# One decoder layer on eight cores: a build-time list scheduler, one matmul less per attention tile, and no activation-table switches

## The chip, the cores and the metric

The kernel runs on all eight cores of one Trainium2 chip, two dies of four cores. Each core does two of the sixteen sequences, with its own copy of the weights and no exchange. The time of one execution is that of its slowest core, in device microseconds (us).

Executions come in two states. In the fast one all cores have the same granted TensorE clock. In the slow one the cores of one die, sometimes of both, show a lower clock and run some per cent longer. Kernels are compared here by their fast executions. Where a kernel had none, I take the die that stayed at its normal clock in a slow execution ("undisturbed die"): for kernels that have both, the two agree to within 0.2%.

PE is TensorE, PEld its weight load, DVE VectorE, ACT ScalarE, POOL GpSimd, SP SyncE. "Clock" is the mean granted TensorE clock, 1.00 being full speed. In a row of groups or of the timeline, L492 is line 492 of that kernel's file, and "out<-in" are the program's names.

## The reference, cut to what matters

```python
xn = rms_norm(h, mix_norm)                       # h: (16, 4096, 1024) float32
z  = xn @ w_in                                   # b, c, u (512 each), q, k, v (512 each), f (8)
y_conv = gate_b * causal_depthwise_conv(gate_c * u, conv_w)       # width 3
log_f  = log_sigmoid(z_f + b_f)
c      = cumsum(log_f)                           # per head, along the sequence
s      = q.k / 8 + c[t] - c[s]                   # causal
y_attn = softmax(s) @ v                          # 8 heads x 64
y  = group_rms_norm(concat(y_conv, y_attn))      # over groups of 64 channels
h  = h + y @ w_o
h  = h + (silu(g) * up) @ w_down                 # g, up = rms_norm(h) @ w_gate_up, 2816 wide
h  = h + sigmoid(rms_norm(h) @ w_ple_gate + b) * (p @ w_ple_proj)
return rms_norm(h)
```

The softmax's denominator is never needed: the group norm that follows takes any factor of a row out again. What matters for time is the term c[t] - c[s]. Its part in s (the key) is one number per partition when a score tile has keys on partitions and queries along the row, so it can be the bias of the exponential. Its part in t (the query) varies along the row. That is the "decay row".

## The kernel before: the parts that matter here

A core works through sixteen blocks of 512 tokens, eight per sequence. The Python loop emits a block's operations in the order of the formula, and each engine executes them in that order: norm, q, k, v, convolution with its group norm, attention, output projection, norm, FFN, norm, embedding gate, final norm.

```python
class Prog:
    def op(self, eng, fn, reads=(), writes=()):       # appended to the engine's queue at once
        deps = self._deps(reads, writes)
        self.cnt[eng] += 1
        tok = (eng, self.cnt[eng])
        self.q[eng].append((fn, deps, None))
        self._update(tok, reads, writes)
        return tok
# ... (cut: DMA, emission with semaphores, constants, buffers)
            # attention: one unit is a head x a tile of 128 keys x 512 queries
            for i in range(len(units) + LOOK):                     # LOOK = 3
                if i < len(units):
                    h, kt, c0, dg, first, last = units[i]          # dg: tile on the diagonal
                    def fqk(e, ...):
                        e.matmul(PS[sbk][:, c0:T], lhsT=KT[:, hp, kt * 128:(kt + 1) * 128],
                                 rhs=QT[:, h, c0:T], start=True, stop=False)
                        ins = e.matmul(PS[sbk][:, c0:T], lhsT=sel[:, h * 128:(h + 1) * 128],   # decay row
                                       rhs=crow[:, c0:T], start=False, stop=(not dg))
                        if dg:
                            ins = e.matmul(PS[sbk][:, c0:c0 + 128], lhsT=identb[:], rhs=maskb[:],
                                           start=False, stop=True)
                        return ins
                    P.op("pe", fqk, ...)
                    P.op("act", lambda e, ...: e.activation(out=Pb[pi][:, c0:T], in_=PS[sbk][:, c0:T],
                         func=AF.Exp, bias=cK[:, kt, h:h + 1], scale=1.0), ...)
                j = i - LOOK
                if j >= 0:
                    P.op("pe", lambda e, ...: e.matmul(PS[ob][0:65, c0:T], lhsT=VA[:, kt, h, :],
                         rhs=Pb[pi][:, c0:T], start=first, stop=last), ...)
# ... (cut: group norm of a head: Square, matmul, Ln, Exp(-0.5 x), multiply; odd heads are moved
#      to partitions 64 to 127 by one more matmul with a shift matrix)
            norm_to_xnT(hb, 8)                                     # root by Ln, then Exp, on ACT
            for (f_lo, f_n, gu, dn) in pl["ffn"]:
                for j in range(f_n):
                    mm_fm(bg, gv, BG, (j % 2) * 128)
                    mm_fm(bu, gv, BG, 256 + (j % 2) * 128)
                    P.op("act", lambda e, ...: e.activation(out=sg[si][:], in_=PS[bg][:], func=AF.Silu), ...)
                    P.op("dve", lambda e, ...: e.tensor_tensor(out=actT[:, j, :], in0=sg[si][:],
                         in1=PS[bu][:], op=ALU.mult), ...)
```

## Time and profile before

| | before |
|---|---|
| median of the first 4 executions | 6063 us (5842 to 6454) |
| fast execution, slowest core | 5842 us |
| profiled core: TensorE busy, idle | 5043 us, 798 us |
| mean clock, fast execution | 0.924 |
| activation-table loads | 65 of 1283 ns |
| share of the weights' DMA queue | 45% of 16 engines |

The prediction below shows the page's head and three stretches of one block. Four more rows of the page's costliest groups (busy us and mean ns of one, then the idle time of that engine just before them and what ended it) carry an argument that it missed:

```profile
L722 ACT ACTIVATE P<-ps,cK 128x512 bf16<-128x512 f32 (+3 forms) x2304 | 1341.5, 650 | 92.6 <-PE ps L715 69.3
...
L713 PE MATMUL ps<-QT,KT 128*128 128x512 bf16 (+3 forms) x2304 | 846.9, 368 | 101.9 <-DVE acc L637 101.9
L732 PE MATMUL ps<-P,VA 128*65 128x512 bf16 (+3 forms) x2304 | 841.0, 365 | 43.6 <-ACT P L722 15.9
L715 PE MATMUL ps<-crow,sel_s 128*128 128x512 bf16 (+3 forms) x2304 | 845.7, 367 | 0.0
```

L713, L715 and L732 are the three matmuls of an attention unit (scores, decay row, values), L722 its exponential. Matmuls overlap in the record, so the mean of 367 ns is not their spacing: that is 0.217 us when dense, 0.65 us for the three of a full tile.

The slices of DVE and ACT (each digit the busy tenths of 1/40 of the span), which show the engines taking turns:

```profile
DVE  3242423222230240331242323241312402313113
ACT  3142342625428148258242524336262382572662
```

### The profile page before, as it was taken

Reading aid. Unit: us, or ns where it says so; the run is one execution under the profiler, and the core shown is the slowest. Engines: PE = TensorE matmul, PEld = TensorE weight load, DVE = VectorE, ACT = ScalarE, POOL = GpSimd, SP = SyncE. Lnnn points to the kernel's source line nnn. Section 1 sums busy time; section 2 is a strip of 40 time slices with the busy share of each in tenths; the row PEclk is TensorE's granted clock in tenths of the full one; section 3 lists DMA queues with packets and bytes.
Section 4 is the critical chain, followed back from the end, with each engine's and each line's share of the span. In section 5 each row is a group of like instructions: output and inputs, shape, how many; then the busy total and the mean of one; then the engine's idle time right before and its main releaser. Section 6 shows DMA issues by size and latency. Waiting matters only on the chain.

```text
span 5840.9 us, 76877 instructions; the slowest of 8 cores (5820.6 to 5840.9 us)
## 1 busy us (share of the span) xinstructions
PE 5043.0 (86%) x24128; PEld 2316.7 (40%) x24128; DVE 1629.1 (28%) x2492; ACT 2552.1 (44%) x4663; POOL 270.7 (5%) x509
## 2 busy tenths in 40 slices
PE   5978788898889989889979798888889899898898
PEld 2433334343444334434434343334444344344443
DVE  3242423222230240331242323241312402313113
ACT  3142342625428148258242524336262382572662
POOL 0000000000000000000000000000000000000000
PEclk9989899998999989999989898989999899899999
DMA  5756638174370650740747474562725607417225
GB/s 106 118 109 105 123 60 153 26 131 86 69 144 15 114 114 3 137 89 6 134 95 133 91 126 100 92 135 43 133 53 102 126 3 137 89 31 127 56 36 111
DMA packets 101977, 534.92 MB, mean 92 GB/s; under 512 B 12768, under 2 KB 21344, under 8 KB 60640
## 3 DMA queue, kind: packets, MB, share of 16 engines
q0 software_dynamic: 72720, 453.75, 45.2%
q1 hardware_dynamic: 28880, 76.26, 3.9%
q8 instruction: 222, 3.64, 0.3%
q14 instruction: 155, 1.27, 0.1%
HBM read 950.13 MB, written 33.55 MB: 168 GB/s over the span
## 4 chain that ended last, share of the span: by engine, by line
PE 69%; DVE 13%; ACT 8%; issue 6%; DMA 4%; DVEq 0%; ACTq 0%; POOL 0%; POOLq 0%
PE ps L492 29%; PE ps L732 8%; PE ps L713 7%; PE ps L715 7%; PE ps L817 7%; DMA wslot<-wpack 4%; DVE xnT L484 4%; PE ps L767 2%; PE ps L771 2%; DVE acc L869 1%; PE ps L543 1%; DVE h L873 1%; ACT acc L867 1%; PE ps L857 1%; ACT sqb L736 1%
## 5 line engine op out<-in xcount | busy, mean ns | idle before, releaser
L492 PE MATMUL ps<-xnT,wslot 128*128 128x512 bf16 x8192 | 1909.5, 397 | 73.8 <-DVE xnT L484 54.3
L722 ACT ACTIVATE P<-ps,cK 128x512 bf16<-128x512 f32 (+3 forms) x2304 | 1341.5, 650 | 92.6 <-PE ps L715 69.3
L492 PEld LDWEIGHTS ps<-xnT,wslot 128*128 128x128 bf16 x8192 | 827.8, 102 | 1136.5 <-issue 259.4
L713 PE MATMUL ps<-QT,KT 128*128 128x512 bf16 (+3 forms) x2304 | 846.9, 368 | 101.9 <-DVE acc L637 101.9
L732 PE MATMUL ps<-P,VA 128*65 128x512 bf16 (+3 forms) x2304 | 841.0, 365 | 43.6 <-ACT P L722 15.9
L715 PE MATMUL ps<-crow,sel_s 128*128 128x512 bf16 (+3 forms) x2304 | 845.7, 367 | 0.0
L817 PE MATMUL ps<-wslot,actT 128*128 128x512 bf16 x2816 | 612.9, 379 | 46.6 <-DVE actT L799 46.6
L382 POOL DMA_DIRECT2D wslot<-wpack x496 | 265.6, 538 | 5522.6 <-PE ps L492 2159.9
L797 ACT ACTIVATE sqb<-ps 128x512 bf16<-128x512 f32 x176 | 105.2, 598 | 834.5 <-PE ps L492 834.4
L817 PEld LDWEIGHTS ps<-wslot,actT 128*128 128x128 bf16 x2816 | 273.2, 98 | 386.3 <-issue 61.5
L732 PEld LDWEIGHTS ps<-P,VA 128*65 128x65 bf16 x2304 | 252.4, 110 | 429.8 <-issue 360.2
L477 PE MATMUL ps<-identb,xnbf 128*128 128x128 bf16 x1536 | 152.5, 262 | 233.7 <-DVE xnT L484 146.9
L444 ACT ACTIVATE junk<-h 128x1024 bf16<-128x1024 f32 x132 | 139.1, 1054 | 448.2 <-DVE h L822 232.9
L715 PEld LDWEIGHTS ps<-crow,sel_s 128*128 128x128 bf16 x2304 | 227.5, 99 | 246.0 <-issue 14.2
L797 ACT ACTIVATE sg<-ps 128x512 bf16<-128x512 f32 x176 | 105.2, 598 | 489.1 <-PE ps L492 489.1
L822 DVE TENSOR_TENSOR h<-h,ps 128x512 f32<-128x512 f32 x256 | 175.9, 687 | 482.9 <-PE ps L817 482.9
L713 PEld LDWEIGHTS ps<-QT,KT 128*128 128x128 bf16 x2304 | 227.2, 99 | 207.9 <-issue 122.0
L857 PE MATMUL ps<-wslot,xnT 128*128 128x512 bf16 x1024 | 269.3, 411 | 22.7 <-DVE pT L840 15.6
L799 DVE TENSOR_TENSOR actT<-sqb,ps 128x512 bf16<-128x512 bf16 x176 | 121.1, 688 | 557.0 <-PE ps L492 540.2
L685 DVE SCALAR_TENSOR_TENSOR yTa<-ps,gattn_s,rs 64x512 bf16<-64x512 f32 x64 | 47.5, 743 | 773.5 <-ACT rs L682 773.5
L799 DVE TENSOR_TENSOR actT<-sg,ps 128x512 bf16<-128x512 bf16 x176 | 121.1, 688 | 488.6 <-PE ps L492 488.6
L689 DVE SCALAR_TENSOR_TENSOR ytmp<-ps,gattn_s,rs 64x512 bf16<-64x512 f32 x64 | 47.5, 742 | 715.8 <-ACT rs L682 380.4
(102 smaller groups left out, 3579.4 us busy)
## 6 DMA issues: line engine op xcount, KB each, us to landing
wslot<-wpack POOLq DMA_DIRECT2D x320, 1024.0 KB, 12.9
wslot<-wpack POOLq DMA_DIRECT2D x64, 768.0 KB, 7.2
wslot<-wpack POOLq DMA_DIRECT2D x64, 640.0 KB, 8.5
h<-x SPq DMA_DIRECT2D x64, 512.0 KB, 19.8
y<-h SPq DMA_DIRECT2D x64, 512.0 KB, 9.0
wslot<-wpack POOLq DMA_DIRECT2D x48, 512.0 KB, 7.1
pin<-p SPq DMA_DIRECT2D x64, 128.0 KB, 4.9
gfin_s<-gfin SPq DMA_DIRECT2D x1, 512.0 KB, 10.1
```

The costliest lines, as they stand in the source:

```text
L382: P.dma("pool", lambda e, o=o, i_=i_: e.dma_start(out=o, in_=i_), f"w{s_}", writes=wr)
L484: P.op("dve", lambda e, pbv=pbv, gb=gb, tt=tt: e.tensor_tensor(out=xnT[:, :, tt * 128:(tt + 1) * 128], in0=pbv.rearrange("p (k t) -> p k t ...
L492: ins = e.matmul(PS[b][:], lhsT=wv[:, kc, c0:c0 + 128], rhs=xnT[:, kc, :], start=(kc == 0), stop=(kc == 7))
L713: e.matmul(PS[sbk][:, c0:T], lhsT=KT[:, hp, kt * 128:(kt + 1) * 128], rhs=QT[:, h, c0:T], start=True, stop=False)
L715: ins = e.matmul(PS[sbk][:, c0:T], lhsT=sel[:, h * 128:(h + 1) * 128], rhs=crow[:, c0:T], start=False, stop=(not dg))
L722: P.op("act", lambda e, sbk=sbk, pi=pi, c0=c0, kt=kt, h=h: e.activation(out=Pb[pi][:, c0:T], in_=PS[sbk][:, c0:T], func=AF.Exp, bias=cK[:, ...
L732: P.op("pe", lambda e, ob=ob, kt=kt, h=h, pi=pi, c0=c0, first=first, last=last: e.matmul(PS[ob][0:65, c0:T], lhsT=VA[:, kt, h, :], rhs=Pb[ ...
L797: P.op("act", lambda e, bg=bg, si=si: e.activation(out=sg[si][:], in_=PS[bg][:], func=AF.Silu), reads=[Bps[bg]], writes=[Bsg[si]])
L799: P.op("dve", lambda e, bu=bu, si=si, j=j: e.tensor_tensor(out=actT[:, j, :], in0=sg[si][:], in1=PS[bu][:], op=ALU.mult), reads=[Bsg[si], ...
L817: ins = e.matmul(PS[b][:], lhsT=actT[:, j, tt * 128:(tt + 1) * 128], rhs=rhs, start=(j == 0), stop=(j == na + nb - 1))
L822: P.op("dve", lambda e, b=b, hh=hh, dh=dh: e.tensor_tensor(out=hh[:, dh * 512:(dh + 1) * 512], in0=hh[:, dh * 512:(dh + 1) * 512], in1=PS[ ...
L857: e.matmul(PS[bgt][:], lhsT=xnT[:, kc, tt * 128:(tt + 1) * 128], rhs=pgv[:, kc, :], start=(kc == 0), stop=False)
```

## The change

The intent has three parts. First, the order of the instructions no longer follows the program: each operation gets a priority ("key") and an estimated duration, and a list scheduler, run while the kernel is built, lays attention and convolution of block n+1 between FFN, embedding and final norm of block n, and the projections of block n+2 at block n's end. Second, the decay row leaves the full tiles. Third, every function on ACT comes from one table set, so that the mixing costs no table loads. The diff's core, with cuts marked:

```diff
+    def op(self, eng, fn, dur, key, reads=(), writes=(), after=(), sem=None, nbytes=0):
+        ...                                   # records the operation, places nothing
+    def schedule(self):
+        ...                                   # per engine: of the ready operations the lowest key,
+        ...                                   # else the one that is ready first; buffers are
+        ...                                   # allotted here; engines and the DMA are simulated
@@ attention, full tiles
-    e.matmul(PS[sbk][:, c0:T], lhsT=KT[...], rhs=QT[...], start=True, stop=False)
-    ins = e.matmul(PS[sbk][:, c0:T], lhsT=sel[...], rhs=crow[:, c0:T], start=False, stop=(not dg))
+    ins = e.matmul(st.ap()[:, c0:T], lhsT=KT[...], rhs=QT[...], start=True, stop=not dg)
+    if dg:
+        e.matmul(st.ap()[:, c0:T], lhsT=sel[...], rhs=crow[:, c0:T], start=False, stop=False)
@@ attention, once per head: before the diagonal tiles are added, multiply by exp(decay of the query)
+    if ui == blk * 4 and blk:
+        P.op("dve", lambda e, ...: e.tensor_tensor(out=o.ap()[0:65, :], in0=o.ap()[0:65, :],
+                                                   in1=et.ap()[0:65, :], op=ALU.mult), ...)
@@ roots: Exp of the float's bits as a first guess, then a polynomial on DVE, instead of Ln and Exp
-    P.op("act", ... func=AF.Ln, scale=1.0 / D, bias=EPS)
-    P.op("act", ... func=AF.Exp, scale=-0.5)
+    P.op("act", ... in_=m.bitcast(I32), func=AF.Exp, scale=SEED_SCALE, bias=SEED_BIAS)
+    P.op("dve", ...)                          # five tiny operations after it, one before
@@ FFN (sigmoid of the embedding gate likewise)
-    P.op("act", ... func=AF.Silu)
+    P.op("act", ... func=AF.Tanh, scale=0.5)
+    P.op("dve", ... scalar_tensor_tensor(out=tb, in0=th, scalar=1.0, in1=PS g, op0=add, op1=mult))
@@ the shift of odd heads
-    P.op("pe", lambda e, ...: e.matmul(PS[g2][:, :], lhsT=shiftm[:, :], rhs=ytmp[:, :], ...))
+    dst = yTa[64:128, h // 2, :]              # DVE writes the upper half itself
@@ weights: 8 slots of 2048 columns instead of 4 of 4096; PSUM: 3 banks scores, 2 output, 3 all else
@@ the order: low key first
+    for n in range(-2, NB):
+        b = float(n)
+        if n >= 0:
+            load_h(n, b - 0.15)
+            wo(n, b + 0.0, b + 0.06)
+        if 0 <= n + 1 < NB:
+            conv(n + 1, b + 0.15, b + 0.7)
+            attention(n + 1, b + 0.0, b + 0.9)
+        if n >= 0:
+            ...                               # norm tiles, b + 0.06
+            ffn(n, b + 0.07, b + 0.68)
+            ...                               # norm tiles, b + 0.68
+            ple(n, b + 0.70, b + 0.80)
+            finish(n, b + 0.80)
+        if n + 2 < NB:
+            qkv(n + 2, b + 0.78, b + 1.0)
```

## The prediction

> **What bounds the kernel now.** I read the cores first: all eight lie within 0.4% of each other, so one core may stand for the chip, and the profile fell in a fast execution (5842 us; the other three took 5998, 6128 and 6454). Then the busy times and the forty slices.
>
> ```profile
> span 5840.9 us, 76877 instructions; the slowest of 8 cores (5820.6 to 5840.9 us)
> ...
> PE 5043.0 (86%) x24128; PEld 2316.7 (40%) x24128; DVE 1629.1 (28%) x2492; ACT 2552.1 (44%) x4663; POOL 270.7 (5%) x509
> ...
> PE   5978788898889989889979798888889899898898
> ...
> PEclk9989899998999989999989898989999899899999
> DMA  5756638174370650740747474562725607417225
> ```
>
> TensorE is the only engine near full. But no slice stays full: it dips, the clock dips with it, and ACT, DVE and DMA take turns. Three stretches of one block, read in the windows view, say why (columns: busy us and count of PE, weight loads, DVE, ACT, POOL, then clock, DMA share, GB/s):
>
> ```profile
> 4860.00:4920.00 60.00, 58.58 (x272) 26.24 (x271) 12.85 (x19) 6.58 (x11) 4.75 (x9) 1.00 0.84 144
> 4980.00:5040.00 60.00, 48.94 (x242) 23.62 (x243) 25.74 (x46) 16.46 (x34) 1.58 (x3) 0.85 0.70 162
> 5100.00:5160.00 60.00, 58.08 (x286) 27.20 (x285) 2.23 (x3) 58.43 (x101) 0.00 (x0) 1.00 0.00 1
> ```
>
> The first is FFN: PE dense at clock 1.00, ACT nearly idle, DMA at 84%. The third is attention: PE dense at 1.00, ACT just as full with exponentials, DMA idle. The middle one is norm, projection and convolution: PE idles a fifth of the time and the clock falls to 0.85. So the limit is PE, plus small serial chains at stage borders that leave it idle and then slow. The waits of PE, longest first, show the chains:
>
> ```profile
> PE ps L477 <- DVE xnT L484: 146.9, 96, 4.2
> PE ps L713 <- DVE acc L637: 101.9, 16, 6.8
> PE ps L477 <- DVE xnbf L460: 85.4, 33, 30.3
> PE ps L696 <- DVE ytmp L689: 81.2, 58, 2.8
> PE ps L644 <- ACT sqb L611: 65.8, 32, 3.1
> ```
>
> Norm transposes, the convolution's last multiply, the shift of odd heads, the group norm: each is PE waiting for a vector or scalar chain with no other PE work queued. The chain of waits agrees: PE is 69% of it, DVE 13%, ACT 8%, DMA only 4%.
>
> To split the span I need PE's work at full clock. In a dense FFN stretch 160 matmuls of 512 columns take 34.7 us: 0.217 us each. Work in units of such a matmul, from the code: per 512-token block 96 for q, k, v, 96 for the convolution's projections, 64 output projection, 528 FFN, 88 embedding gate, 16 for means and shifts, so 888, times 16 blocks 14,208; attention's 1792 full tiles take 3 each (scores, decay row, values), 5376; 512 diagonal tiles of mean width 320 take 3 x 0.625, 960, and masks 128; 1664 transposes a quarter each, 416. Sum 21,088 x 0.217 = 4575 us, and about 50 for small fp32 and 8-column matmuls: 4625. The span is thus 4625 of work, 5841 - 5043 = 798 of idle, and the rest, about 418, of matmuls stretched by the lower clock.
>
> **What the Trainium skill says.** "TensorE: Matmul & The Clock Gate", Part 1: the array runs at half clock until it has been busy for a window of about 3.4 us, and falls back after idling. The trace agrees: the first matmuls after the start follow each other at 0.43 us, dense ones at 0.217. The same page, "Seeing it yourself": a current limit takes a die to 13/16 of the clock when three or more of its cores run dense matmuls. This profile doesn't show it: dense stretches on eight cores have 1.00. The slower executions may be it; I can't tell from a fast profile. "ScalarE: Activation LUTs", Table sets: exp and tanh share a set, ln and exp another, and a switch needs a load. The trace has 65 loads of 1283 ns, 83 us in all. "SBUF — State Buffer", Who interferes with whom: VectorE in its two-port modes locks GpSimd out, and with it the descriptors of GpSimd's DMAs. No row here shows such a stall.
>
> **The change part by part.** It turns the kernel's order over to a list scheduler that runs when the kernel is built. Operations carry a priority and an estimated duration; each engine's static order comes from that simulation. Attention of block n+1 and its convolution are laid beside FFN, embedding and final norm of block n.
>
> 1. Decay row. For full tiles the second matmul (decay of the query) goes; exp of it multiplies the accumulated output once per head before the diagonal tiles. Gone: 1792 x 0.217 = 389 us of PE, all on the path, since attention is PE-dense. Added: 8 matmuls, 8 ACT exponentials (0.59 each) and 8 DVE multiplies (0.69) in 14 blocks: 24 us of PE.
>
> 2. Odd-head shift: 64 matmuls gone, 14 us; its 81 us of waits go too. The convolution's epsilon row adds 64 back. V and the embedding gate run as 256-column halves: same columns, 3072 instructions; as 128-column transposes run at 66 ns in the trace when warm, I add 30 us for small-matmul loss.
> PE work after: 14,208 + 112 + 3584 + 960 + 128 + 416 = 19,408 x 0.217 = 4211, plus 50 and 30: 4290 us. That is 335 less than before.
>
> 3. Tables. Silu and sigmoid become tanh; ln/exp roots become an exponential of the float's bits plus two polynomial corrections on DVE. All but one or two of the 65 table loads go (83 us of ACT), which is what makes interleaving exp and FFN possible.
>
> 4. DVE pays. Per block, with rows' durations: norms 12 x (0.75 + 1.22 + about 0.85 for six tiny operations), 34; 12 group roots at 4 x 0.72 + 0.75 final, 44; convolution's products 4 x 3.4, 13; FFN 22 x 1.4, 31, and down-projection sums 16 x 0.72, 12; embedding 8 x 1.44, 12; output sums 5.5; gate logarithm by polynomial, 26 x 0.26, 7; casts of q, k, v 8; decay multiply 5.5; final norm 4 x 2.1, 8; chaining gaps of 0.1 us, 10. About 190 us, or 3040 in all against 1629.
>
> 5. ACT: 83 us fixed per block and 22 x blk for exponentials, so 2560, unchanged (loads and Ln out, tanh equal to silu, new exponentials in).
>
> 6. DMA: the same weights in half-size pieces, double the slots, all issues including x and y on GpSimd's queue, x read twice. Busy share before is 49% of 5841, 2870 us; 34 MB more at the 76 MB per 228 us of the old queue add 100: 2970.
>
> 7. Idle. Of 798 idle plus 418 clock loss, most sits at borders that now have the other block's matmuls to fill them. What cannot be filled: start (38 us until the first projection, as before), the first block's projection, convolution and attention with no FFN beside them (about 40), the last block's norms and output (about 25). I call it 100. Within the middle I allow 5 to 6% of 4290, 240 us, for in-order queues meeting durations the scheduler did not foresee.
>
> Sum in a fast execution: 4290 + 100 + 240 = 4630, that is 0.79 of 5842.
>
> **The rivals.**
> DVE becomes the bound in light blocks. With blk = 0 PE has about 888 + 75 + 8 units, 210 us; DVE 190, 90% of it, in order, on three PSUM banks shared by FFN, convolution and norms. For: FFN's gate now needs ACT, then DVE, then DVE before its banks are free. Against: at blk = 7 PE has 310 us. If every light block (four of sixteen) went to 240 us and the next four lost 15, I would see 4630 + 150 = 4780.
> DMA becomes the bound: 2970 us of 4630 is 64%, in light blocks 185 of 210. One GpSimd queue with x, y and weights in order could hold a load behind a store. Against: smaller pieces, and demand spread over the whole block instead of bursts at 84%. It would add to the same light blocks, 4750 to 4850.
> The clock: if eight denser cores trip the limit of 13/16, 4290 / 0.8125 = 5280, and the time is 5300 to 5400, still under before's fast time. Against: 1.00 in all dense stretches of this profile.
> The optimistic one: the scheduler fills almost all, 3% loss: 4290 + 100 + 130 = 4520.
>
> **Range and chances.** Fast 4630. The median of before's executions is 1.04 of its fast one; a kernel with a larger share of dense matmuls will suffer a slow die at least as much, so its median may be 1.04 to 1.06, 4815 to 4910. I predict 4740, between the fast time and such a median. The range 4450 to 5150 holds the optimistic and both stall rivals, and a moderately slow state; only the full clock limit falls outside. Even that is faster than before, so faster by over 2%: 0.96; within 2%: 0.02; slower: 0.02, for an order that serializes on a wait I have not seen.
>
> **What would show it.** Right: PE at 94% or more of the span in the middle; clock near 1.00 in a fast execution; slices of ACT and DVE level instead of taking turns; matmuls of the decay row only in diagonal tiles; one or two table loads; DVE near 3000 us, ACT near 2550; the chain of waits over 85% PE. Wrong: PE holes ended by DVE operations of the gate product or root correction in each sequence's first blocks (DVE bound); holes ended by weight transfers (DMA bound); clock at 0.81 on all cores while PE is full (current limit); or PE work well over 4290, which would mean that short matmuls cost more than I took.

## The result, and the profile after

The changed kernel took 5055 us (median of 12 executions, 4833 to 5585), the kernel before 5998 us (median of 17). Its fast executions are at 4833 to 4837 us, those of before at 5840 to 5848. The ratio of fast executions is 0.829 (95% interval 0.825 to 0.833): faster. A ratio here is the mean time of one kernel's fast executions over the other's of the same rounds, so not quite the ratio of the medians quoted.

The first profile fell in a slow execution. It shows what slow means: two stretches of one core (windows view; the columns are those of the prediction's table) in which PE is full, with two clocks:

```profile
300.00:360.00 60.00, 60.00 (x230) 24.94 (x229) 27.05 (x40) 7.70 (x13) 8.15 (x18) 0.81 0.77 121
2580.00:2640.00 60.00, 60.00 (x294) 27.97 (x293) 33.76 (x51) 14.07 (x26) 9.55 (x20) 1.00 0.81 134
```

On this core dense stretches have 0.81 until about 1460 us and 1.00 after that; other cores have their 0.81 at the end.

So I profiled the changed kernel once more as it was. The page of that fast execution (span; busy us, share and count; then slices of PE, DVE, ACT, clock and DMA; then the shares of the chain of waits):

```profile
span 4832.4 us, 74571 instructions; the slowest of 8 cores (4817.3 to 4832.4 us)
...
PE 4413.1 (91%) x23548; PEld 2244.0 (46%) x23984; DVE 2676.2 (55%) x5380; ACT 2279.9 (47%) x4209; POOL 625.2 (13%) x1234
...
PE   4798989989899999998989989898999999989988
...
DVE  3656565554645545446575665756555455464454
ACT  2323344544555646556233333535455465565641
...
PEclk9898999999999999999999999999999999999999
DMA  7486876666656665566676777666665655555555
...
PE 78%; DVE 8%; issue 7%; ACT 5%; DMA 1%; DVEq 0%; POOL 0%; ACTq 0%; POOLq 0%
```

Against the page of before: DVE (0 to 4 tenths before) and ACT (1 to 8) no longer take turns but lie at 3 to 7 and 1 to 6, DMA lies at 4 to 8 throughout instead of swinging from 0 to 8, PE and its clock have lost most of their dips, and the chain is 78% PE instead of 69%. (This core's record lacks 436 matmuls. Another core of the same execution, 4821.7 us long, has them: PE busy 4439, idle 383. The sums below use it; its windows view of the whole span:)

```profile
0.00:4833.00 4833.00, 4439.08 (x23984) 2241.25 (x23984) 2676.03 (x5380) 2280.52 (x4209) 623.98 (x1234) 0.97 0.67 117
```

I cut a core's span into stretches of 2 us, and in each took PE's busy and idle time and the granted clock. Busy time times (1 - clock) is what the low clock added to matmuls; the rest of busy is work at full speed.

| us, one core of a fast execution | before | after | difference |
|---|---|---|---|
| PE work at full speed | 4742 | 4341 | -401 |
| added by the lower clock | 301 | 98 | -203 |
| PE idle | 798 | 383 | -415 |
| span | 5841 | 4822 | -1019 |

So some 40% of the gain is work that went; 60% is idle time filled, and the clock that came back with it. The split is good to some 4%: experiment 9, with the same instructions in another order, has 4306 us of "work", 35 less, so this row also holds small losses that the record counts as busy.

What idle is left? The windows view of two stretches (columns: us; busy and count of PE, PEld, DVE, ACT, POOL; clock, DMA share, GB/s):

```profile
2780.00:2800.00 20.00, 7.00 (x29) 3.48 (x30) 17.55 (x51) 4.79 (x12) 4.49 (x8) 0.57 1.00 230
2880.00:2900.00 20.00, 19.60 (x95) 8.91 (x94) 11.19 (x17) 6.53 (x11) 2.30 (x5) 1.00 0.66 108
```

The second is a normal stretch: PE 98% busy at full clock. The first is the border between two blocks early in a sequence, where attention is short and nothing of it is left as filler. DVE has 17.55 of 20 us to do, PE 7, and the clock is at 0.57. The timeline of that border (start, duration, what, and in brackets the idle time before it and what ended it):

```profile
2782.24 2.48 DVE L1056 SCALAR_TENSOR_TENSOR h<-h,stat,gfin_s 128x1024 f32<-128x1024 f32 x2
...
2790.83 1.42 DVE L602 TENSOR_SCALAR xnbf<-xs,stat 128x1024 bf16<-128x1024 f32 x2
...
2791.72 1.87 PE L611 MATMUL ps<-identb,xnbf 128*128 128x128 bf16 x16 [10.16 <-DVE xnbf L602]
...
2796.69 0.15 PEld L565 LDWEIGHTS ps<-xnTq,wslot 128*128 128x128 bf16 x1 [0.28 <-issue]
2797.11 0.15 PEld L565 LDWEIGHTS ps<-xnTq,wslot 128*128 128x128 bf16 x1 [0.28 <-issue]
2797.54 0.15 PEld L565 LDWEIGHTS ps<-xnTq,wslot 128*128 128x128 bf16 x1 [0.28 <-issue]
```

Final norms of the old block (L1056) and the tiny operations of three norms come first in DVE's static order. Only then does DVE write the tile that PE's transposes need (L602). PE has waited 10.16 us and pays again afterwards: its weight loads follow each other every 0.42 us, half speed, until about 2800. Such borders top PE's list of waits (us in total, times, longest):

```profile
PE ps L611 <- DVE xnbf L602: 77.5, 30, 26.5
PE ps L833 <- ACT P L846: 73.9, 85, 4.5
PE ps L718 <- DVE fst L714: 34.1, 16, 3.0
PE ps L611 <- DVE stat L577: 27.2, 2, 23.0
```

L611 is the transposes of a norm, L833 the scores of an attention unit waiting for a bank that an exponential has yet to read, L718 the cumulated gate at the end of DVE's gate polynomial. The longest waits of the first and the fourth row, 26.5 and 23.0 us, are the start of the kernel.

### The profile page after: what moved, and what is told of

Its sections match the earlier page's. It is cut to its first block, busy times and chain, and to the rows that moved or that the text cites. A ratio compares the mean times of both kernels' runs of the same rounds, so it can differ in the third digit from the quotient of the medians.

```text
span 5013.9 us, 75007 instructions; the slowest of 8 cores (4908.1 to 5013.9 us)
## 1 busy us (share of the span) xinstructions
PE 4656.7 (93%) x23984; PEld 2305.7 (46%) x23984; DVE 2680.5 (53%) x5380; ACT 2286.1 (46%) x4209; POOL 626.8 (13%) x1234
## 4 chain that ended last, share of the span: by engine, by line
PE 81%; DVE 7%; issue 6%; ACT 4%; DMA 1%; DVEq 0%; POOL 0%; ACTq 0%; POOLq 0%
PE ps L565 55%; PE ps L833 8%; PE ps L792 8%; PE ps L1031 4%; ACT xnbf L595 2%; ACT P L846 1%; PE ps L611 1%; PE ps L836 1%; PE ps L673 1%; DMA xs<-x 1%; PE ps L1026 1%; PE ps L838 0%; DVE h L1056 0%; DVE ac L901 0%; DVE xnbf L602 0%
## 5 line engine op out<-in xcount | busy, mean ns | idle before, releaser
L846 ACT ACTIVATE P<-ps,bK 128x512 bf16<-128x512 f32 (+3 forms) x2304 | 1374.4, 654 | 877.3 <-PE ps L833 557.9
L565 PE MATMUL ps<-xnTd,wslot 128*128 128x512 bf16 x5632 | 1352.0, 394 | 10.3 <-DVE ac L904 3.2
L833 PE MATMUL ps<-QT,KT 128*128 128x512 bf16 (+3 forms) x2304 | 861.1, 379 | 72.7 <-ACT P L846 68.2
L565 PEld LDWEIGHTS ps<-xnTd,wslot 128*128 128x128 bf16 x5632 | 559.7, 100 | 716.7 <-issue 245.0
L565 PE MATMUL ps<-xnTq,wslot 128*128 128x512 bf16 x2560 | 637.6, 410 | 20.0 <-DVE xnTq L616 16.1
L973 DVE SCALAR_TENSOR_TENSOR tb<-th,ps 128x512 bf16<-128x512 f32 x352 | 241.6, 686 | 632.1 <-ACT th L970 630.7
L970 ACT ACTIVATE th<-ps 128x512 f32<-128x512 f32 x352 | 210.1, 597 | 627.1 <-PE ps L565 616.4
L565 PEld LDWEIGHTS ps<-xnTq,wslot 128*128 128x128 bf16 x2560 | 264.1, 104 | 361.8 <-issue 169.6
L833 PEld LDWEIGHTS ps<-QT,KT 128*128 128x128 bf16 x2304 | 232.0, 101 | 403.6 <-issue 256.5
L977 DVE TENSOR_TENSOR actT<-tb,ps 128x512 bf16<-128x512 bf16 x352 | 241.6, 686 | 179.6 <-PE ps L565 173.0
L1031 PE MATMUL ps<-wslot,xnTd 128*128 128x256 bf16 x2048 | 259.8, 283 | 0.0
L611 PE MATMUL ps<-identb,xnbf 128*128 128x128 bf16 x1536 | 126.6, 236 | 140.9 <-DVE xnbf L602 76.6
L1031 PEld LDWEIGHTS ps<-wslot,xnTd 128*128 128x128 bf16 x2048 | 207.5, 101 | 52.4 <-issue 9.2
L611 PEld LDWEIGHTS ps<-identb,xnbf 128*128 128x128 bf16 x1536 | 105.9, 106 | 179.3 <-issue 165.3
```

Of the source, the lines that this page charges most:

```text
L565: ins = e.matmul(out, lhsT=l, rhs=r, start=(i0 + i == 0), stop=(i0 + i == n - 1))
L611: ins = e.transpose(out=pv[:, kc * 128:(kc + 1) * 128], in_=xb.ap()[:, kc * 128:(kc + 1) * 128], identity=identb[:])
L833: ins = e.matmul(st.ap()[:, c0:T], lhsT=KT[:, hp, kt * 128:(kt + 1) * 128], rhs=QT[:, h, c0:T], start=True, stop=not dg)
L846: P.op("act", lambda e, st=st, pt=pt, c0=c0, kt=kt, h=h: e.activation(out=pt.ap()[:, c0:T], in_=st.ap()[:, c0:T], func=AF.Exp, bias=bK[:, ...
L970: P.op("act", lambda e, tg=tg, th=th: e.activation(out=th.ap()[:], in_=tg.ap()[:], func=AF.Tanh, scale=0.5), 0.6, k - 0.1, reads=[tg], wri ...
L973: P.op("dve", lambda e, tg=tg, th=th, tb=tb: e.scalar_tensor_tensor(out=tb.ap()[:], in0=th.ap()[:], scalar=1.0, in1=tg.ap()[:], op0=ALU.ad ...
```

## The experiments

The prediction was right, so the questions were which part of the change earns what, whether the accounting of the prediction holds, and what stands between 4833 us and the 4630 us that it gave a fast execution. All kernels gave correct results. Times are of fast executions unless said otherwise. The scheduler runs anew for every variant of the changed kernel, so each edit also moves other instructions; how much of a small difference (experiments 5, 6 and 10) is that, no run shows.

**1. The changed kernel again**, unchanged, for a profile.

> The changed kernel once more, unchanged, to get a profile of an undisturbed die: the first profile fell in a slow execution (die clocks 0.92 and 0.945). If its time is PE work of about 4290 us plus holes, a fast profile of 4833 us shows a clock of 0.97, PE busy 4450 to 4550 us and holes of 280 to 380 us, of which about 60 before the first projection. If the work itself was under-counted (rival), PE is busy 4600 us or more at the same clock and holes are under 230.

Measured: 4834 us, PE busy 4439 us with 383 us of idle on a core with a complete record, clock 0.97. Busy lies just below what was expected and idle just above. Close enough that the accounting by work, clock and idle stands.

**2. The kernel before with only the decay row gone** from its full tiles; order, tables and shift as before. The value matmuls of diagonal tiles come two units later, so that the multiply on the output has time, with six probability buffers instead of four.

```diff
-                        e.matmul(PS[sbk][:, c0:T], lhsT=KT[...], rhs=QT[:, h, c0:T], start=True, stop=False)
-                        ins = e.matmul(PS[sbk][:, c0:T], lhsT=sel[...], rhs=crow[:, c0:T],
-                                       start=False, stop=(not dg))
+                        ins = e.matmul(PS[sbk][:, c0:T], lhsT=KT[...], rhs=QT[:, h, c0:T], start=True,
+                                 stop=(not dg))
                         if dg:
+                            e.matmul(PS[sbk][:, c0:T], lhsT=sel[...], rhs=crow[:, c0:T],
+                                     start=False, stop=False)
...
+                    if kt == blk * 4 - 1:
+                        P.op("dve", lambda e, ob=ob: e.tensor_tensor(out=PS[ob][0:65, :],
+                             in0=PS[ob][0:65, :], in1=et[0:65, :], op=ALU.mult), ...)
```

> The kernel before with the decay matmul taken out of full tiles and nothing else changed (order, tables and norms as before). Theory 'the two halves need each other': in the old order attention has only ACT beside PE, and its exponentials (0.59 us a full tile, ACT 58 of 60 us busy) become the bound, so of 389 us of PE work at most 100 come off: 5740 to 5840 us fast, 0.98 to 1.00. Rival 'PE work counts wherever it is': 365 us come off, 5480 us, 0.94.

All four executions were slow. In two of them one die kept its clock, at 5784.6 and 5785.7 us; undisturbed dies of before are at 5831 to 5842, typically 5837. So 52 us, 0.9%, for 1792 matmuls that the prediction put at 389 us, 365 net of what is added. The windows view of attention at full clock, from its profile:

```profile
5460.00:5520.00 60.00, 54.39 (x230) 17.00 (x230) 4.33 (x7) 59.69 (x109) 0.00 (x0) 1.00 0.00 1
5520.00:5580.00 60.00, 52.92 (x220) 16.53 (x218) 5.00 (x7) 59.65 (x110) 0.00 (x0) 1.00 0.00 1
```

ACT is busy 59.7 of 60 us, PE has idle time that it can't use. The exponential now sets the pace: the 168 full-width ones of these two stretches take 99.2 us, 0.59 each, where three matmuls took 0.65. That is 0.06 us for each of 1792 tiles, 108 us; the 112 new exponentials of the query's decay take 0.59 us each on the same engine, 66 us. The 42 us left, an estimate, fit the 52 measured. In the old order the removed matmul was nearly free.

**3. The changed kernel with the decay row back** in all full tiles, and its scheduler told so.

```diff
-            if ui == blk * 4 and blk:
+            if False:                             # no multiply of the output
...
-                                   start=True, stop=not dg)
+                                   start=True, stop=False)
+                    ins = e.matmul(st.ap()[:, c0:T], lhsT=sel[...], rhs=crow[:, c0:T],
+                                   start=False, stop=not dg)
```

> The changed kernel with the decay matmul back in every full tile (and the row factor on the output gone). Theory 'PE is the bound nearly everywhere in the new order': 365 us of PE work come back in full, 4833 + 340 to 400 = 5170 to 5230 us fast, 0.885 to 0.895 of before. Rival 'holes and the chains of ACT and DVE set the time': the holes of 7% swallow most of it, under 5000 us, below 0.855.

Measured: 5085 and 5088 us, ratio to before 0.871 (0.869 to 0.874). That is 252 us slower than the changed kernel, between the two theories. On one core PE's work is up by 318 us, while its idle time falls from 383 to 327 us: part of the extra work filled holes that would have been empty. So the row is worth five times more in the new order than in the old. The reason is in part argued: attention's exponentials now run beside matmuls of the FFN, and no longer pace PE except for 74 us of waits (L833 on L846 above; 50 us with the row back). The row is not worth its whole length as long as there are holes.

**4. The changed kernel with the overlap's priority taken away**: attention and convolution of block n+1 rank behind everything of block n.

```diff
-            conv(n + 1, b + 0.15, b + 0.7)
-            attention(n + 1, b + 0.0, b + 0.9)
+            conv(n + 1, b + 0.82, b + 0.86)        # moved below finish(n)
+            attention(n + 1, b + 0.86, b + 0.97)
-            qkv(n + 2, b + 0.78, b + 1.0)
+            qkv(n + 2, b + 0.98, b + 1.0)
```

> The changed kernel with the priorities of convolution and attention of the next block put behind the end of this block's output, so that the scheduler only takes them where nothing else is ready. Theory 'the deliberate laying of attention beside the FFN is what counts': attention is ACT-bound again (0.59 against 0.43 us of PE a full tile, 290 us) and DMA and DVE chains lie bare at the borders: 5200 to 5500 us fast, 0.89 to 0.94. Rival 'any order that fills gaps does it': within 2% of the changed kernel, under 4930 us, 0.845.

Six executions, none with both dies at their normal clock (one of 5179 us is labelled fast, but both its dies have 0.92). Undisturbed dies took 4987 to 4996 us at clock 0.97, some 156 us over the changed kernel's 4832. That is again between the theories, and near the rival. It tells something about the scheduler: a low priority does not keep an operation out of a hole. Whenever nothing better is ready, the simulation takes what is; in one stretch of the profile (4120 to 4140 us, core 4) PE is full and ACT has four exponentials of attention beside four tanh of the FFN. Without the chosen priorities some 850 of 1005 us of gain remain. How much of that is filled holes and how much removed work, this run does not say; the new instructions in the old order were not run.

**5. x and y on SyncE's queue** instead of GpSimd's, three lines.

```diff
-            P.dma("pool", lambda e, xt=xt, r0=r0: e.dma_start(out=xt.ap()[:], in_=x_d[...]),
+            P.dma("sp", lambda e, xt=xt, r0=r0: e.dma_start(out=xt.ap()[:], in_=x_d[...]),
```

> The changed kernel with x (both loads) and y issued by SyncE instead of GpSimd's queue, which then carries only weights and the embedding rows. Theory 'start only': the third and fourth tile of x no longer sit behind nine weight loads, the first projection starts at about 40 us instead of 64.6, and nothing else changes: 15 to 30 us less, 4803 to 4818 on an undisturbed die. Rival 'the one queue also holds up block borders': more than 60 us less, under 4770.

Measured: 4825 and 4829 us, 7 us less (4 to 12 by the extremes): less than expected. The first projection came at 59.9 instead of 64.6 us. One queue for everything was no bound.

**6. Shorter DVE chains.** A norm's root from six tiny operations to three (scale and constants folded into others), the gate polynomial from fourteen to eight by taking add and multiply in one instruction.

```diff
-        P.op("dve", ... m = m * (1.0 / D) + EPS)
...
-        P.op("dve", ... m = m * a); P.op("dve", ... m = m * a)
-        P.op("dve", ... bb = m * RC2 + RC1); P.op("dve", ... bb = bb * m)
-        P.op("dve", ... m = (bb + RC0) * a)
+        P.op("dve", ... m = (m * a) * a)
+        P.op("dve", ... m = (m + RC1 / RC2) * m)
+        P.op("dve", ... m = (m + RC0 / RC2) * a)
...
-        for k in (11, 9, 7, 5, 3, 1):
-            dv(... d_ = d_ * c_)
-            dv(... d_ = d_ + 1.0 / k)
+        for k in (13, 11, 9, 7, 5, 3):
+            dv(... d_ = (d_ + 1.0 / k) * c_)
```

> The changed kernel with the tiny serial DVE operations shortened: 3 instead of 6 per norm tile (256 tiles), 8 instead of 14 in the gate's polynomial (16 blocks); about 14 us of DVE per block with their gaps. Same PE work, same priorities. Theory 'the holes at block borders, 213 us on one core, are DVE's pile of small chains (DVE 70% busy there against 51% elsewhere)': 80 to 150 us less, 4680 to 4750. Rival 'borders wait for order, banks or transfers, not for DVE': less than 25 us, over 4805.

Measured: 4780 and 4782 us, ratio to before 0.818 (0.816 to 0.821); 54 us less than the changed kernel, between theory and rival. DVE's busy time fell by 96 us to 2580, PE's idle time by 43 us. The chains on DVE are part of the remaining loss, but a small part: most of their length already lay beside PE work.

**7. Silu back in the FFN**, one ACT operation in place of tanh and a DVE operation; 352 DVE operations of 0.69 us fewer.

```diff
-                P.op("act", ... func=AF.Tanh, scale=0.5)
-                P.op("dve", ... scalar_tensor_tensor(out=tb, in0=th, scalar=1.0, in1=tg, op0=add, op1=mult))
+                P.op("act", ... func=AF.Silu)
```

> The changed kernel with Silu itself for the FFN gate in place of tanh and one DVE operation (240 us of DVE saved). Theory 'tanh is what allows exp and FFN to share ACT': up to 700 table loads of 1.28 us come in, ACT goes from 2280 to about 3000 us or more, and gates come late: over 5000 us. Rival 'ACT is half idle and hides the loads': within 2%, under 4930.

Measured: 5042 us in the one fast execution, 208 us more, though DVE's busy time fell from 2676 to 2443 us. The groups of its profile that account for nearly all of the 465 loads (count, busy us, mean ns, idle before):

```profile
L970 ACT ACT_TABLE_LOAD x232 | 297.7, 1283 | 168.1 <-PE ps L565 160.4 <-remote 6.1
L846 ACT ACT_TABLE_LOAD x170 | 218.1, 1283 | 27.9 <-PE ps L833 10.6 <-PE ps L838 9.5 <-PE ps L792 1.4
L857 ACT ACT_TABLE_LOAD x59 | 75.7, 1283 | 15.7 <-PE ps L804 8.8 <-PE ps L913 6.2
```

A Silu (L970) among exponentials (L846, L857) costs a load there and one back. The changed kernel has a single load. The DVE operation that the change pays is the cheaper price: the mixing is cheap only with one function set, as the prediction's step 3 says. (The scheduler was not told of the loads; an order that gathers the Silus might lose less, and was not tried.)

**8. One PSUM bank moved** from the scores (3 to 2) to everything else (3 to 4), since all projections, FFN and norms share three.

```diff
-    qS = Pool("S", banks[0:3])
-    qO = Pool("O", banks[3:5])
-    qD = Pool("Dn", banks[5:8])
+    qS = Pool("S", banks[0:2])
+    qO = Pool("O", banks[2:4])
+    qD = Pool("Dn", banks[4:8])
```

> The changed kernel with one PSUM bank moved from the score tiles (3 to 2) to the dense groups (3 to 4). Theory of the prediction's first rival 'three banks for FFN, convolution and norms hold PE': over 1% faster, under 4785. Otherwise no gain or slower, as two score banks leave ACT's exponentials less lead: 4820 to 5000.

Measured: 4897 us in the one fast execution, 63 us more. In this order the scores need their third bank more than the rest needs a fourth. This does not show that three are plenty for the rest, as both changed at once.

**9. Other priorities only.** Searching the keys for the shortest span in the scheduler's own simulation gave these; the instructions are the same.

```diff
-            wo(n, b + 0.0, b + 0.06)
+            wo(n, b + 0.062, b + 0.079)
-            conv(n + 1, b + 0.15, b + 0.7)
-            attention(n + 1, b + 0.0, b + 0.9)
+            conv(n + 1, b + 0.11, b + 0.711)
+            attention(n + 1, b + -0.072, b + 0.863)
-            ffn(n, b + 0.07, b + 0.68)
+            ffn(n, b + 0.252, b + 0.693)
-            ple(n, b + 0.70, b + 0.80)
-            finish(n, b + 0.80)
+            ple(n, b + 0.792, b + 0.848)
+            finish(n, b + 0.849)
-            qkv(n + 2, b + 0.78, b + 1.0)
+            qkv(n + 2, b + 0.78, b + 0.94)
```

(and load_h from b - 0.15 to b - 0.192)

> The changed kernel with other priorities only, same operations: FFN held back against attention (starts at 0.25 of a block instead of 0.07), embedding gate and output moved to 0.79 to 0.85 so that they lie beside the next block's projections, attention from -0.07 to 0.86. Theory 'the holes at borders come from the order: no PE work is left to lay over the norms': holes of one core fall from 383 to under 230 us and the clock loss, which follows the holes, from 148 to under 110; 4620 to 4690 us. Rival 'DVE's pile at the borders sets them whatever the order': over 4780.

Measured: 4649 and 4650 us, clock 0.979: 184 us less, as expected in time, though not in where it came from. On one core idle falls from 383 to 270 us, not to under 230, and the clock's part from 98 to 71. Two rows of its waits, to be set beside those above:

```profile
PE ps L611 <- DVE xnbf L602: 65.1, 39, 26.0
PE ps L833 <- ACT P L846: 10.6, 27, 1.1
```

The wait for norms at the borders, on which the theory rested, fell by only 12 us; that of scores for exponentials fell by 63. The largest single remaining loss of the change lay in numbers that nobody had tuned.

**10. The start.** Experiment 5, and besides it the first block's V weights and the residual copy of x are issued behind its four x tiles. It is the kernel's start that this is about; in the first profile after the change (slow, but the start is not affected) the timeline shows a square of x waiting 27.78 us for its tile, and the first projection:

```profile
51.37 1.06 ACT L595 ACTIVATE xnbf<-xs 128x1024 bf16<-128x1024 f32 x1 [27.78 <-DMA xs<-x]
...
64.59 10.72 PE L565 MATMUL ps<-xnTq,wslot 128*128 128x512 bf16 x32 [1.58 <-DVE stat L582]
```

```diff
-        wv = [wload(g, L(0.35)) for g in plan["v"]]
+        wv = [wload(g, L(0.35), xl if m == 0 else ()) for g in plan["v"]]     # xl: the x loads
...
-                  key + 0.001 * tt, f"h{tt}", 128 * 4096, writes=[Bh[tt]])
+                  key + 0.001 * tt, f"h{tt}", 128 * 4096, writes=[Bh[tt]], after=first_x if n == 0 else ())
```

> The changed kernel with x and y on SyncE and, in the first block only, V's weights and the residual's x issued after the four tiles of x. Theory 'the start waits for x behind 4.5 MB of weights and residual': the first projection starts at 35 to 42 us instead of 64.6 and the time falls by 20 to 30 us, to 4802 to 4812. Rival 'the weights of K set it': under 10 us.

Measured: 4818 and 4821 us, 15 us less; the first projection at 48.0 us. Right in direction, half in size.

**11. The parts that helped, together**: 6, 9 and 10.

> All that helped together: short small chains, x and y on SyncE with the first block's V weights and residual loads issued after x, and the other priorities. If the gains add: 4530 to 4600 us, 0.775 to 0.79 of before; if short chains bring nothing once the order covers them: 4610 to 4660.

Measured: 4568 to 4573 us in five fast executions of seven, median of all seven 4570 us, clock 0.98. Before had only one fast execution in those rounds, too few for a ratio with an interval; against before's usual fast time it is 4570 / 5840 = 0.783, against the changed kernel 0.945. This beats both, and the gains add: 54, 184 and 15 make 253 us, 264 were measured. Its page and the first rows of PE's waits:

```profile
span 4567.6 us, 73199 instructions; the slowest of 8 cores (4558.7 to 4567.6 us)
...
PE 4362.6 (96%) x23984; PEld 2248.5 (49%) x23984; DVE 2564.1 (56%) x4518; ACT 2277.3 (50%) x4209; POOL 532.7 (12%) x1042
...
PE   6899999999999999999999999999999999999998
```

```profile
PE ps L610 <- DVE xnbf L601: 70.6, 48, 23.5
PE ps L721 <- DVE fst L717: 42.9, 12, 4.7
```

PE is at nine tenths or more in every slice but the first two and the last. Idle is 205 us, the clock's part 66. A third of what remains of the first wait is one wait of 23.5 us, for the kernel's first x tile.

**12. That best version with the decay row back.**

> The best version with the decay matmul back in every full tile. In the old order the matmul was worth 52 us, in the changed one 252 of 365. Theory 'its worth grows with how much of the time PE is the only bound': with fewer holes left to hide it, 310 to 365 us come back, 4878 to 4933 on an undisturbed die. Rival 'about 110 us of it always lie in attention stretches that ACT paces': 230 to 270, 4800 to 4840.

Measured: 4929 us, clock 0.981: 359 us more, of the 365 us that the prediction gave the row. The idle time that is left is not filled by it (207 us with the row, 205 without), so PE pays for every matmul.

| decay row in full tiles | without | with | its cost |
|---|---|---|---|
| order of before (undisturbed dies) | 5785 | 5837 | 52 |
| order of the change | 4834 | 5086 | 252 |
| tuned order | 4570 | 4929 | 359 |

## Why the prediction was right, and where it was off

**Time and range.** 4740 us was predicted, in a range of 4450 to 5150; the median was 5055, inside, and faster as expected. It gave a median 1.04 to 1.06 of the fast time, and 5055 / 4834 is 1.046. That is in part luck: the median hangs on how many executions are slow. The first four were all slow, with a median of 5224, outside the range; and the medians of the variants above lie at 1.00 to 1.08 of their fast times. The fast time is the better test. The point lies low because it was put between a fast time and a median, and because the fast time itself, 4630, was 204 us too low.

**PE's work**: 4290 against 4341 measured at full speed, 1.2% low. For before, 4625 against 4742, 2.5% low, which is why its clock loss of 418 us was really 301. Counting matmuls in units of 0.217 us is a good method, and the fall was underrated (335 against 401), not overrated.

**Decay row, "all on the path, since attention is PE-dense"**: wrong for the old order, as experiment 2 shows. The line of the profile that has PE at 58.08 of 60 us has ACT at 58.43; the prediction says so, and prices only PE. Within the changed kernel it costs 252 of 365 us; only where no holes are left is it the full sum.

**Tables**: right, and experiment 7 puts a number on it: 208 us if a single function of another set stays.

**DVE and ACT**: 3040 predicted, 2676 measured; 2560 predicted, 2280 measured. They were overestimated by 14% and 12%, so the rival of a DVE bound in light blocks got more room than it deserved. It is there in part, in the border stretch shown above, for 10 to 20 us at a time, not for whole blocks. The shorter chains of experiment 6 gave 54 us.

**DMA as a bound**: no. The queue has 64% of 16 engines' time, but PE of the slowest core waits for a transfer only once, 2.8 us, and moving x and y to another queue gave 7 us. What the prediction missed is the start: "38 us until the first projection, as before" was 64.6, since the third x tile waited 27.78 us while weights went first in the one queue; issuing those later brought it to 48.0 in experiment 10. The first 300 and the last 60 us together cost some 112 us of idle against the 100 allowed.

**The mis-sized term: idle and what follows it.** The prediction allowed 100 for the ends and 240 for the middle, 340 in all, and expected a clock "near 1.00". Measured are 383 of idle and, on top, 98 us of matmuls stretched by the clock that fell in and after those holes: 481. That is 141 of the 192 us by which the 4822 us of this core exceed 4630; the other 51 are work. The allowance of 5 to 6% for the middle counted what the holes would be, not what PE pays after them: for before the prediction lists idle and clock loss side by side, for after it sums only idle. The page of before held the rate: 301 us of stretch for 798 of idle, 0.38 us for each. After, it is 98 for 383, 0.26; in the best version 66 for 205, 0.32. At 0.3, an estimate from these three, the 340 of idle would have asked for some 100 more.

**The signs.** PE has 94% of the span from 200 to 4620 us on one core, just what was named. The chain was to be over 85% PE and is 78%.

**The full clock limit** (5300 to 5400): not in fast executions. There every stretch of 5 us that follows 10 us of dense matmuls has 1.00, some 470 to 510 of them on each of the eight cores. In slow executions the limit did come, as 0.81 in dense stretches. Executions with a die at a mean of 0.80 to 0.81 took 5548 to 5585 us, more than the rival said, which left out most of the idle time.

What stays open: why one execution is slow and another not; what the scheduler alone is worth, apart from the new instructions; how much of the 205 us of idle time in the best version a better order could still fill, as the search was short; and what a fourth bank would give if the scores kept three.

## What to carry to other kernels

Before pricing a removed instruction, look which other engine is equally full in that stretch: a matmul that was worth 52 us behind an exponential was worth 359 us once independent matmuls filled the queue. A scheduler that fills holes kept most of the gain here even with poor priorities, and good ones were then the cheapest knob left: taking the overlap's priority away cost 156 us, tuning a dozen numbers won 184. When you estimate idle time, add what the clock takes with it, in these kernels 0.26 to 0.38 us for each us of idle.

## What the Trainium skill lacked or had wrong

- "TensorE: Matmul & The Clock Gate", Part 1, has the limit of 13/16 set in within 5 to 20 us of a third core of a die running dense matmuls, and hold while the load lasts. The size agrees: dense stretches of slow executions have 0.81. What the page lacks is that a kernel on all eight cores can escape it: in the fast executions dense stretches have 1.00 on each core from start to end (mean 0.969 after, 0.982 in the best version). Whether three cores of a die were dense at the same moment there is not shown, as each core's trace counts from its own start. What the page says of the half clock after idling agrees: after a hole of 10.16 us the weight loads came every 0.42 us instead of 0.217.
- "ScalarE: Activation LUTs", What ACT_TABLE_LOAD costs, gives 1283 ns for a load, which the loads of experiment 7 confirm, and 2.66 us for a switch with its drain. In the time of the whole kernel a load cost 0.45 us (208 / 465, net of the 352 DVE operations saved): most of it lay beside PE work or was offset by them. ACT's busy time rose by 586 us, 1.26 us per load.
- No page gives a rate for idle time of PE in a mixed schedule. The three kernels examined for it here show 0.26 to 0.38 us of stretched matmuls per us of idle.
